# Equal byte offsets for TensorE's operands, value products of two heads at once, and stages in another order

## The chip, the core and the metric

One Trainium2 chip; the kernel runs on one of its cores. The metric is device microseconds from launch to end of the whole program, as the median of several runs. TensorE (PE) multiplies into PSUM, VectorE (DVE), ScalarE (ACT) and GpSimd (POOL) do elementwise work, and SyncE (SP), ACT and POOL issue DMA transfers from queues of their own.

## The reference

One decoder layer on a sequence of 1024 tokens of width 1024, all in float32.

```
u    = rmsnorm(x) * (1 + scale(c)) + shift(c)
proj = u @ w_in                       # a, b, conv_gate: 1024 columns each; q, k, v, ret_gate: 1024 each
conv = silu(layernorm(causal_conv31(a * sigmoid(b)))) @ conv_pw * silu(conv_gate)
q, k = rotary(q), rotary(k) / 16      # 4 heads of 256
r    = retention(q, k, v)             # per head, with decay, in chunks of tokens
ret  = head_groupnorm(r) * silu(ret_gate)
h    = x + gate(c) * (concat(conv, ret) @ w_out)
out  = rmsnorm(h) * final_g
```

## The kernel before

Every float32 operand of a product is split into a high part in TensorE's float32r format and a low remainder (`split`: a ScalarE copy and a subtraction). A product is then three matmuls per 128 rows of contraction: high by high, high by low, low by high (`mm3`, lines 81 to 83). One of the two operands is stationary (the weights of the matmul instruction, 128x128), the other streams through (the moving operand, 128x512 or 128x256).

The work runs in stages, each of which leaves intermediate results in DRAM buffers (`d_y`, `d_v`, `d_qk`, ...):

- **Head** (`head`): loads, the RMS norm, transposes, the modulation from c, and four 128-column products that start while u is still being made (`ps_e`, `ps_paa` to `ps_pdd`). Then two more products, w_s (`ps_s`), whose weights are split on POOL (`lo_s`).
- **Pairs** (`pair`): the rest of the projection with a seven-product scheme over 2x2 blocks (tiles `pa`, `pb`, `pd`; weights `ph`, `pl`; moving operands `uh`, `ul`, `th`, `tl`). DVE meanwhile runs the convolution, 30 tap instructions per channel tile (`conv_taps`, L263), for eight tiles; the last one, `y7`, is worked on when the pairs are done.
- **Values of head 0** (`values_ps`, tiles `ps_v`, weights `wvh`, `wvl`), stored to `d_v` and loaded back.
- **Retention** (`retention`), for four heads in four chunks each: loads of q, k, v and the gate, splits of them on ACT and DVE (`qch`/`qcl`, `kch`/`kcl`, `vch`/`vcl`), scores `sp`, output `op`, state update `up`, group norm, transposes `tp`. All its matmuls have 256 or 128 moving columns, and each chunk is a chain over PE, DVE, ACT and POOL.
- Between the heads stand the **values of the next head** (`values`), after head 0 the statistics of the layer norm (`ln_stats`: each of the eight rows of `d_y` is loaded, shifted by the mean, stored again, squared and summed; then 1/sqrt and a broadcast `rbs`), and after head 2 the normalisation `norm_z` of those rows, which makes zh and zl in the buffers that uh and ul held.
- **Pointwise** products (`pointwise`, tiles `ps_pw`) of zh and zl, and the **output** products (tiles `ps_o`, and `ps_ol` for the last 128 tokens).

The order on each engine is made when the program is built: the Tile planner takes instructions by priority (the order of the code, shifted by `high_priority` offsets) and puts each on its engine in one fixed sequence. An engine then runs its sequence strictly in order. The addresses in SBUF follow from the pools' order and sizes.

Of the kernel before, what the change touches and what calls it, by code (L numbers as in the profile page):

```python
# [7 lines left out]
F32 = mybir.dt.float32  # L8
F32R = mybir.dt.float32r
# [14 lines left out]
PAD_RIGHT = 8  # L24
# [22 lines left out]
def hybrid_layer(ctx: ExitStack, tc: tile.TileContext, x, vec, c_row, ada_ss, ada_g, adab_g, w_e, w_s, w_p, w_v,  # L47
# [17 lines left out]
    d_v = dram.tile([H, P, TT, 2 * P], F32, name="d_v")  # L65
# [62 lines left out]

    pad_p = ctx.enter_context(tc.tile_pool(name="pad", bufs=1, side="right"))
    pad_p.tile([P, PAD_RIGHT], F32, name="pad")  # L130
# [14 lines left out]
    def head():  # L145
# [104 lines left out]
        return ps  # L250

    def conv_taps(m, ap=None, yp=None):

        with tc.high_priority(offset=-TAPS_LATER):
# [11 lines left out]
            nc.sync.dma_start(d_y[m], y)  # L266
# [16 lines left out]
    def values_ps(ws, name):  # L283

        for tg in range(2):
            ps = [mmp.tile([P, 2, 2 * P], F32, tag="mm", name=f"ps_{name}{tg}{i}") for i in range(2)]
            for k in range(KT):
                wh, wl = ws[k]
                for j in range(4):
                    sl = slice((4 * tg + j) * P, (4 * tg + j + 1) * P)  # L290
                    mm3(ps[j // 2][:, j % 2], uh[k][:, sl], ul[k][:, sl], wh, wl,
                        k == 0 and j % 2 == 0, k == KT - 1 and j % 2 == 1)
            for i in range(2):
                yield 2 * tg + i, ps[i]

    early = head()
# [26 lines left out]
    for j, n in enumerate(STD):  # L323
        ps = unit(*load_w(w_s[j], [P, KT, P], f"s{n}", sw, nc.gpsimd), uh, ul, f"s{n}")
        if j == 0:
            gate_out(n, ps)
# [5 lines left out]
    with tc.tile_pool(name="one", bufs=1, reuse_waits="tile") as op_, \  # L332
# [162 lines left out]
        for h in range(1):  # L495
            ws = []
            for j in range(4):
                raw = op_.tile([P, HK, P], F32, tag="raw", name=f"wv{h}{j}", bufs=6)
                nc.sync.dma_start(raw, w_v[h, j // 2][:, 2 * (j % 2):2 * (j % 2) + 2].rearrange(
                    "p k (a c) -> p (k a) c", a=2))  # L500
                hi = op_.tile([P, HK, P], F32R, tag="ph", name=f"wvh{h}{j}", bufs=7)
                lo = op_.tile([P, HK, P], F32R, tag="pl", name=f"wvl{h}{j}", bufs=7)
                split(hi, lo, raw, nc.gpsimd)
                ws += [(hi[:, 2 * i:2 * i + 2], lo[:, 2 * i:2 * i + 2]) for i in range(2)]
            for n, ps in values_ps(ws, f"v{h}"):
                vs = snap(ps, f"v{h}{n}")
                nc.scalar.dma_start(d_v[h, :, 2 * n:2 * n + 2], vs.rearrange("p (t e) -> p t e", t=2))
# [6 lines left out]
    with tc.tile_pool(name="ret", bufs=1, reuse_waits="tile") as rp, \  # L514
            tc.tile_pool(name="retps", bufs=1, space=bass.MemoryType.PSUM) as rps:

        def ln_stats():
# [7 lines left out]
            for m in range(KT):  # L525
# [6 lines left out]
                else:  # L532
                    sq = fo.tile([P, S], F32, tag="xh", name=f"sq{m}", bufs=2)
                    nc.scalar.activation(sq, yt, AF.Square)
                    nc.vector.tensor_tensor(ysum, ysum, sq, op=ADD)
            var = mmp.tile([P, TT], F32, tag="mm", name="var")
# [15 lines left out]
        def values(h):  # L552
            ws = [load_w(w_v[h, g], [P, 4, 2 * P], f"v{h}{g}", wpool) for g in range(2)]
            ws = [(ws[k // 4][0][:, k % 4], ws[k // 4][1][:, k % 4]) for k in range(KT)]
# [123 lines left out]
        def pointwise(m):  # L678
# [3 lines left out]
            for i in range(2):  # L682
                sl = slice(i * HALF, (i + 1) * HALF)
                nc.vector.tensor_tensor(cg[:, sl], ps[i], cg[:, sl], op=MUL)  # L684
# [214 lines left out]
```

## Time and profile before

| | |
|---|---|
| median of 3 runs | 1012.49 us (1011.83 to 1013.82) |
| the profiled execution | 1015.1 us, of it 1013.3 us from the first to the last instruction (the span) |
| PE busy in the span | 961.0 us, 95% |
| DVE, ACT, POOL busy | 741.1, 412.4, 379.9 us |
| mean granted TensorE clock | 0.975 |

Matmuls overlap: a record of a 512-column matmul lasts about 0.39 us while the next starts about 0.23 us after it. So PE's busy share says whether matmuls follow each other, and the number of matmuls in a stretch says how fast. Times inside the execution are counted from the span's start.

### The profile page before, as it was taken

The numbers are of one execution on the slowest core, as the hardware profiler recorded it, in microseconds if no ns is written. First come the engines' busy times: TensorE is split into PE (matmuls) and PEld (weight loads), VectorE is DVE, ScalarE is ACT, GpSimd is POOL, SyncE is SP. The second block draws the span as 40 slices with busy tenths as digits, with TensorE's granted clock in tenths as the row PEclk, the third lists the DMA queues.
The fourth block names the chain that finished last, engine by engine and source line by source line (L and its number), as shares of the span: only waits on it lengthen the run. The fifth ranks groups of instructions, "written<-read, shape, count | busy, mean of one in ns | idle before, by whom it ended". The sixth has DMA issues, their size and how long they took to land.

```text
span 1013.3 us, 13308 instructions
## 1 busy us (share of the span) xinstructions
PE 961.0 (95%) x4880; PEld 812.2 (80%) x4880; DVE 741.1 (73%) x926; ACT 412.4 (41%) x676; POOL 379.9 (37%) x347
## 2 busy tenths in 40 slices
PE   7899999999999999999977977899999999999997
PEld 5687788888888888888877966899888878888886
DVE  6989889898999999999799569536785354422322
ACT  7754443434333342433334556546742323211110
POOL 3201989878879778877402010101101000000000
PEclk9999999999999999999997996899999999999999
DMA  9712333324243353352256577445776577332111
GB/s 358 295 63 73 104 115 135 114 83 144 93 138 118 112 181 105 103 167 94 96 178 208 189 255 261 173 146 185 219 258 236 191 243 225 125 104 84 62 42 42
DMA packets 83827, 154.99 MB, mean 153 GB/s; under 512 B 6705, under 2 KB 40241, under 8 KB 82610
## 3 DMA queue, kind: packets, MB, share of 16 engines
q1 hardware_dynamic: 81026, 148.64, 44.2%
q10 hardware_dynamic: 2736, 5.51, 1.4%
q8 instruction: 38, 0.62, 0.3%
q14 instruction: 27, 0.22, 0.1%
HBM read 107.99 MB, written 46.14 MB: 152 GB/s over the span
## 4 chain that ended last, share of the span: by engine, by line
PE 32%; DMA 9%; DVE 7%; ACT 2%; issue 2%; POOL 0%; POOLq 0%; DVEq 0%; ACTq 0%; SPq 0%
PE ps_o L83 5%; PE ps_o L81 5%; PE ps_o L82 5%; DVE y L263 3%; PE ps_pw L81 2%; PE ps_pw L83 2%; PE ps_pw L82 2%; PE ps_v L81 1%; PE ps_v L82 1%; PE ps_v L83 1%; DMA v<-d_v 1%; DMA yt<-d_y 1%; DMA ys<-d_y 1%; DMA d_y<-ys 1%; DMA d_v<-vs 1%
## 5 line engine op out<-in xcount | busy, mean ns | idle before, releaser
L263 DVE SCALAR_TENSOR_TENSOR yp<-a,vec_t,yp 128x1024 f32<-128x1024 f32 x210 | 269.5, 1283 | 11.5 <-ACT yp L261 7.1
L371 POOL TENSOR_TENSOR pl<-pr,ph 128x512 fp32r<-128x512 f32 x63 | 83.4, 1332 | 94.4 <-ACT ph L370 90.7
L371 POOL TENSOR_TENSOR pl_s<-sm_s,ph_s 128x512 fp32r<-128x512 f32 x63 | 85.7, 1362 | 29.2 <-ACT ph_s L370 26.1
L370 ACT CAST ph_s<-sm_s 128x512 fp32r<-128x512 f32 x63 | 39.0, 622 | 105.8 <-PE pa L82 99.6
L650 POOL TENSOR_TENSOR rs<-mv,kc_t 128x2 f32<-128x2 f32 x16 | 5.5, 344 | 202.1 <-DVE mv L647 171.3
L772 POOL TENSOR_TENSOR fr<-fr,mhalf 128x1 f32<-128x1 f32 x7 | 3.8, 544 | 198.8 <-DVE fr L771 198.8
L370 ACT CAST ph<-pr 128x512 fp32r<-128x512 f32 x63 | 38.8, 622 | 75.7 <-PE pa L82 33.7
L81 PE MATMUL pa<-th,ph_s 128*128 128x512 f32 x168 | 66.1, 393 | 1.0 <-ACT ph_s L370 1.0
L83 PE MATMUL pa<-th,pl_s 128*128 128x512 f32 x168 | 66.2, 394 | 0.7 <-POOL pl_s L371 0.7
L82 PE MATMUL pa<-tl,ph_s 128*128 128x512 f32 x168 | 65.8, 392 | 0.0
L81 PE MATMUL pb<-uh,ph_s 128*128 128x512 f32 x168 | 65.4, 389 | 0.0
L83 PE MATMUL pb<-uh,pl_s 128*128 128x512 f32 x168 | 65.4, 389 | 0.0
L82 PE MATMUL pb<-ul,ph_s 128*128 128x512 f32 x168 | 65.4, 389 | 0.0
L376 POOL TENSOR_TENSOR sm_s<-pr,pr 128x512 f32<-128x512 f32 x42 | 56.4, 1344 | 4.1 <-PE pa L83 2.2
L81 PE MATMUL ps_v<-hi_v,uh 128*128 128x256 f32 x192 | 54.7, 287 | 0.9 <-ACT hi_v L69 0.9
L83 PE MATMUL ps_v<-hi_v,ul 128*128 128x256 f32 x192 | 55.5, 290 | 0.0
L82 PE MATMUL ps_v<-lo_v,uh 128*128 128x256 f32 x192 | 55.0, 287 | 0.0
L763 DVE TENSOR_TENSOR g<-ps_o,gate 128x512 f32<-128x512 f32 x14 | 9.7, 691 | 60.4 <-PE ps_o L83 60.3
L82 PE MATMUL ps_pw<-zl,hi_pw 128*128 128x512 f32 x128 | 50.8, 398 | 0.1
L83 PE MATMUL ps_pw<-zh,lo_pw 128*128 128x512 f32 x128 | 50.8, 399 | 0.0
L81 PE MATMUL ps_pw<-zh,hi_pw 128*128 128x512 f32 x128 | 50.3, 399 | 0.3 <-DVE cgl L684 0.3
L81 PE MATMUL ps_o<-woh,hi_yr 128*128 128x512 f32 x112 | 44.7, 399 | 0.0
(440 smaller groups left out, 2910.7 us busy)
## 6 DMA issues: line engine op xcount, KB each, us to landing
pr<-w_p SPq DMA_DIRECT2D x84, 256.0 KB, 2.7
aw<-ada_ss SPq DMA_DIRECT2D x8, 1024.0 KB, 8.0
d_qk<-ro SPq DMA_DIRECT2D x16, 512.0 KB, 3.1
wo<-w_out SPq DMA_DIRECT2D x16, 512.0 KB, 4.6
xt<-x SPq DMA_DIRECT2D x8, 512.0 KB, 6.5
d_y<-y SPq DMA_DIRECT2D x8, 512.0 KB, 3.4
d_sg<-o SPq DMA_DIRECT2D x16, 256.0 KB, 2.1
q<-d_qk SPq DMA_DIRECT2D x16, 256.0 KB, 4.1
```

The source lines that it names most:

```text
L81: nc.tensor.matmul(ps, lh, rh, start=start, stop=False, skip_group_check=more)
L82: nc.tensor.matmul(ps, lh, rl, start=False, stop=False, skip_group_check=more)
L83: nc.tensor.matmul(ps, ll, rh, start=False, stop=stop, skip_group_check=more)
L263: nc.vector.scalar_tensor_tensor(acc, ap[:, j:j + S], col(V_CW, m * CW + j), acc, op0=MUL, op1=ADD)
L370: nc.scalar.copy(hi, src)
L371: nc.gpsimd.tensor_tensor(lo, src, hi.bitcast(F32), op=SUB)
L376: nc.gpsimd.tensor_tensor(out, a, b, op=op)
L650: nc.gpsimd.tensor_tensor(rs, mv[:, :, 1], kc_t[:, K_G2 + 2 * h:K_G2 + 2 * h + 2], op=MUL)
L763: nc.vector.tensor_tensor(g[:, :n], ps(), gate[:, sl], op=MUL)
L772: nc.gpsimd.tensor_tensor(r, r, mhalf[:, 0:1], op=ALU.pow)
```

## The change

Five things are done at once.

1. **Addresses.** Pools are padded and opened in another order, and placeholder tiles come first in the retention's pool, so that both operands of every float32r matmul start at one offset within 512 bytes. In the two built programs these offsets are:

| products | stationary, before | moving, before | after, both |
|---|---|---|---|
| early head products (`ps_e` and the others of the head) | 320 | 128 | 128 |
| `ps_s` | 192 | 128 | 128 |
| pairs, retention, values of head 0 | 128 | 128 | 128 |
| values of heads 1 to 3 | 128 | 448 | 128 |
| `ps_pw`, `ps_o`, `ps_ol` | 448 | 128 | 128 |

2. **Values.** w_v is laid out for two heads at a time, so one product has 512 moving columns instead of 256: 384 matmuls in place of 768. The values of heads 0 and 1 are all made after the pairs (192 matmuls, weights in th and tl, which the last pair has done with), those of heads 2 and 3 in two halves after heads 0 and 1.
3. **Order of the stages.** The layer norm's squares stay after head 0, its scale and `norm_z` come after head 1 instead of heads 0 and 2, and the pointwise products follow on from there.
4. **Loads and stores.** w_s comes in one load after most of the head's loads, into a buffer of the head. The values of heads 0 and 1, and the last row of `d_y`, are stored from POOL's queue.
5. **The gate** (`gate_step`) is written after the first output tile, and its product takes PSUM from another pool.

```diff
-PAD_RIGHT = 8
+PAD_SW = 24
+PAD_W = 88
...
-    d_v = dram.tile([H, P, TT, 2 * P], F32, name="d_v")
+    d_v = dram.tile([2, P, TT, HALF], F32, name="d_v")
...
+    whp = head_ctx.enter_context(tc.tile_pool(name="wh", bufs=2))
     hp = head_ctx.enter_context(tc.tile_pool(name="head", bufs=1))
-    whp = head_ctx.enter_context(tc.tile_pool(name="wh", bufs=2))
...
+    xs_p.tile([P, PAD_SW], F32, name="pads")
...
+        raw = hp.tile([P, len(STD), D], F32, tag="aw", name="raw_s", bufs=3)
+        nc.sync.dma_start(raw, w_s)
+        ws = []
+        for j, n in enumerate(STD):
+            hi = sw.tile([P, KT, P], F32R, tag="hi", name=f"hi_s{n}")
+            lo = sw.tile([P, KT, P], F32R, tag="lo", name=f"lo_s{n}")
+            split(hi, lo, raw[:, j].rearrange("p (k c) -> p k c", k=KT), nc.gpsimd)
...
-            nc.sync.dma_start(d_y[m], y)
+            (nc.gpsimd if yp is None else nc.sync).dma_start(d_y[m], y)
...
+    def values_ps(t, ws, name):
+
+        ps = mmp.tile([P, HALF], F32, tag="mm", name=f"ps_{name}{t}")
+        sl = slice(t * P, (t + 1) * P)
+        for k in range(KT):
+            mm3(ps, uh[k][:, sl], ul[k][:, sl], *ws[k], k == 0, k == KT - 1)
+        return ps
...
+        for k in range(KT):
+            raw = op_.tile([P, HALF], F32, tag="raw", name=f"wv0{k}", bufs=6)
+            nc.sync.dma_start(raw, w_v[0, k // 2][:, k % 2])
+            hi, lo = (t[:, k % HK] for t in ((th[2], tl[2]), (th[3], th[4]))[k // HK])
+            split(hi, lo, raw, nc.gpsimd)
+            ws.append((hi, lo))
+        for t in range(0, TT, 2):
+            vs = op_.tile([P, 2, HALF], F32, tag="ro", name=f"vs0{t}", bufs=2)
+            for i in range(2):
+                ps = values_ps(t + i, ws, "v0")
+                if t + 2 < TT:
+                    nc.scalar.copy(vs[:, i], ps)
+                else:
+                    nc.vector.tensor_copy(vs[:, i], ps)
+            values_out(0, t, vs, nc.gpsimd)
...
+    pad_p = ctx.enter_context(tc.tile_pool(name="pad", bufs=1, side="right"))
+    pad_p.tile([P, PAD_W], F32, name="padw")
...
+        for tag, n, dt, bufs in (("vs", HALF, F32, 3), ("state", HALF, F32, 1), ("sth", HALF, F32R, 2),
+                                 ("stl", HALF, F32R, 2), ("ob", HALF, F32, 2), ("rn", CH, F32, 2), ("yn", CH, F32, 2),
+                                 ("sh", 3 * P, F32R, 2), ("sl", 3 * P, F32R, 2), ("sm", 3 * P, F32, 1),
+                                 ("gap", P, F32, 1)):
+            rp.tile([P, n], dt, tag=tag, name=f"first_{tag}", bufs=bufs)
...
+        def values(ts):
+
+            if not w_v1:
+                for j in range(4):
+                    hi, lo = load_w(w_v[1, j], [P, 2, HALF], f"v1{j}", wpool)
+                    w_v1.extend((hi[:, i], lo[:, i]) for i in range(2))
+            for t in ts:
+                vs = rp.tile([P, 1, HALF], F32, tag="vs", name=f"vs{t}", bufs=3)
+                nc.scalar.copy(vs[:, 0], values_ps(t, w_v1, "v1"))
+                values_out(1, t, vs, nc.scalar)
...
         for h in range(H):
             retention(h)
-            if h < H - 1:
-                values(h + 1)
+            if h < 2:
+                values(range(h * HK, (h + 1) * HK))
             if h == 0:
-                rbs = ln_stats()
-            if h == H - 2:
+                ln_squares()
+            if h == 1:
+                rbs = ln_scale()
                 for m in range(KT):
                     zh[m], zl[m] = norm_z(m)
```

Three places of the built programs' order matter below. The first is DVE at the border between the pairs' stage and the retention; `y7` are taps of the last convolution tile, `q00`, `k00`, `v00` belong to head 0, chunk 0. Before:

```order
L263 SCALAR_TENSOR_TENSOR y7_2389<-a7_2386,vec_t_75,y7_2389 128x1024 x11
L70 TENSOR_TENSOR qcl00_4641<-q00_4613,qch00_4640 128x512
L70 TENSOR_TENSOR vcl00_4622<-v00_4619,vch00_4621 128x512
L263 SCALAR_TENSOR_TENSOR y7_2389<-a7_2386,vec_t_75,y7_2389 128x1024
L70 TENSOR_TENSOR kcl00_4637<-k00_4615,kch00_4636 128x512
```

In the changed program DVE's rows there are:

```order
L271 SCALAR_TENSOR_TENSOR y7_2384<-a7_2381,vec_t_75,y7_2384 128x1024 x17
L516 COPY vs06_4551<-ps_v06_4552 128x512
L516 COPY vs06_4551<-ps_v07_4578 128x512
L71 TENSOR_TENSOR vcl00_4647<-v00_4644,vch00_4646 128x512
L71 TENSOR_TENSOR qcl00_4666<-q00_4638,qch00_4665 128x512
L71 TENSOR_TENSOR kcl00_4662<-k00_4640,kch00_4661 128x512
```

All taps now stand ahead of the retention's first split, and between them the two copies of the last value tiles.

The second place is PE at the start of head 1 (`sp10` are scores of head 1, chunk 0). Before, transposes of head 0 and the next chunk's scores follow:

```order
L82 MATMUL sp10_5412<-qcl10_5409,kch10_5404 128x128
L660 MATMUL tp03_5041<-ident_t_76,rn030_5042 128x128 x2
L660 MATMUL tp03_5041<-ident_t_76,rn031_5046 128x128 x2
L83 MATMUL sp10_5412<-qch10_5408,kcl10_5405 128x128
L592 MATMUL kp10_5395<-ident_t_76,k10_5383 128x128 x2
L81 MATMUL sp11_5522<-qch11_5518,kch11_5514 128x256
```

In the changed program value products of heads 2 and 3 (`ps_v14`, then `ps_v15`) follow, 29 matmuls in a row, of which these are the first:

```order
L84 MATMUL sp10_5312<-qch10_5308,kcl10_5305 128x128
L82 MATMUL ps_v14_5726<-hi_v10_5084,uh0_94 128x512
L83 MATMUL ps_v14_5726<-lo_v10_5085,uh0_94 128x512
L84 MATMUL ps_v14_5726<-hi_v10_5084,ul0_102 128x512
L82 MATMUL ps_v14_5726<-hi_v10_5084,uh1_95 128x512
```

So independent products now stand inside head 1; over that head they are 96 matmuls of 512 columns.

The third place is SP's queue in the head. Before, the two loads of w_s stand ahead of the fourth `aw` load:

```order
L157 DMA aw_394<-ada_ss 128x2048
L297 DMA kc_t<-kc 128x24
L74 DMA raw_s_705<-w_s 128x1024
L74 DMA raw_s_765<-w_s 128x1024
L157 DMA aw_434<-ada_ss 128x2048
```

In the changed program the one load stands behind the eighth:

```order
L157 DMA aw_591<-ada_ss 128x2048
L162 DMA wer_553<-w_e 128x512
L251 DMA raw_s<-w_s 128x2048
L162 DMA wer_593<-w_e 128x512
L372 DMA pr_11_909<-w_p 128x512
```

The split of w_s moves with it: POOL makes `lo_s` when the seventh of the eight u tiles is being made, not the second.

## Rows read from the trace of the kernel before

**Rows 1.** Busy time in chosen stretches: us, instructions (x), granted TensorE clock, DMA.

```profile
core 0: us, PE busy (x) PEld busy (x) DVE busy (x) ACT busy (x) POOL busy (x), PEclk, DMA share, GB/s
120.00:490.00 370.00, 370.00 (x1634) 306.39 (x1633) 352.45 (x353) 144.04 (x242) 298.91 (x228) 1.00 0.37 120
508.00:524.00 16.00, 16.00 (x135) 16.00 (x135) 15.71 (x16) 4.05 (x8) 0.00 (x0) 1.00 0.62 194
525.00:552.00 27.00, 15.06 (x88) 13.65 (x87) 25.14 (x37) 10.92 (x20) 4.49 (x5) 0.75 0.62 205
525.00:827.00 302.00, 270.77 (x1737) 243.70 (x1735) 194.92 (x337) 149.61 (x246) 34.28 (x66) 0.93 0.64 213
587.00:650.00 63.00, 46.79 (x274) 41.54 (x273) 46.99 (x92) 35.52 (x64) 9.72 (x18) 0.78 0.76 261
650.00:712.00 62.00, 61.76 (x524) 61.56 (x524) 32.73 (x62) 34.94 (x58) 4.78 (x13) 1.00 0.46 145
655.00:669.00 14.00, 14.00 (x122) 14.00 (x121) 3.20 (x5) 4.27 (x8) 0.00 (x0) 1.00 0.35 112
792.00:824.00 32.00, 32.00 (x139) 25.79 (x138) 14.65 (x17) 10.75 (x11) 0.00 (x0) 1.00 0.74 250
827.00:984.00 157.00, 157.00 (x673) 126.34 (x672) 52.76 (x63) 30.54 (x46) 3.27 (x6) 1.00 0.35 116
984.00:1013.30 29.30, 22.25 (x145) 19.87 (x143) 8.55 (x17) 3.80 (x11) 1.27 (x3) 0.96 0.09 36
```

**Rows 2.** DVE in order of time, 490 to 552 us: start, us, tile, count.

```profile
515.87 14.48 DVE L263 SCALAR_TENSOR_TENSOR y<-a,vec_t,y 128x1024 f32<-128x1024 f32 x11
530.27 0.69 DVE L70 TENSOR_TENSOR qcl<-q,qch 128x512 fp32r<-128x512 f32 x1
...
543.26 1.27 DVE L263 SCALAR_TENSOR_TENSOR y<-a,vec_t,y 128x1024 f32<-128x1024 f32 x1
```

**Rows 3.** The chain that ended last, in order of time: start, us, step.

```profile
551.69 0.74 PE ps_v L81 x4
...
591.67 1.15 DVE ys L528
592.84 6.37 DMA d_y<-ys
599.26 5.21 DMA ys<-d_y
```

**Rows 4.** DVE in order of time: last square added, and rows normalised.

```profile
631.71 1.21 DVE L535 TENSOR_TENSOR ysum<-ysum,sq 128x1024 f32<-128x1024 f32 x1
...
650.52 2.36 DVE L671 TENSOR_TENSOR yt<-yt,rbs 128x1024 f32<-128x1024 f32 x2 [2.51 <-ACT rbs L549]
...
706.84 2.35 DVE L671 TENSOR_TENSOR yt<-yt,rbs 128x1024 f32<-128x1024 f32 x2
```

**Rows 5.** The instructions of line 671 (`norm_z`): count, ns, first start to last end.

```profile
L671 DVE TENSOR_TENSOR yt<-yt,rbs x8: 1218/1225/1227, 650.5 to 735.1; 128x1024 f32<-128x1024 f32 x8
```

**Rows 6.** DVE in order of time in the head.

```profile
30.64 3.38 DVE L206 TENSOR_TENSOR ul<-xs,uh 128x1024 fp32r<-128x1024 f32 x1
34.05 2.75 DVE L309 TENSOR_TENSOR xs<-xs 128x512 f32<-128x512 f32 x1
...
39.13 1.22 DVE L206 TENSOR_TENSOR ul<-xs,uh 128x1024 fp32r<-128x1024 f32 x1
...
40.87 0.68 DVE L309 TENSOR_TENSOR xs<-xs 128x512 f32<-128x512 f32 x1
```

**Rows 7.** POOL in order of time in the head.

```profile
30.50 5.76 POOL L70 TENSOR_TENSOR lo_s<-raw_s,hi_s 128x1024 fp32r<-128x1024 f32 x2 [11.21 <-ACT hi_s L69]
```

**Rows 8.** PE's waits, 15 to 115 us: in total, times, longest.

```profile
PE ps_e L82 <- DVE ul L206: 3.0, 2, 2.9
```

**Rows 9.** DMA issues: KB each, median us from issue to landing.

```profile
v<-d_v SPq DMA_DIRECT2D x16, 256.0 KB, 3.6
...
d_v<-vs ACTq DMA_DIRECT2D x12, 256.0 KB, 3.1
```

More of the change, by code (lines that the diff above doesn't have):

```diff
@@ L281, in conv_early, with values_out @@
         return ap
[L283 to L296, printed above, removed]
+    def values_ps(t, ws, name):
[4 more added lines that the diff above has]
+        return ps
+    def values_out(g, t, vs, eng):
+        eng.dma_start(d_v[g, :, t:t + vs.shape[1]], vs)
+    early, w_std = head()
     nc.sync.dma_start(kc_t, kc)
@@ L550, in ln_stats @@
             return rbs
-        def values(h):
-            ws = [load_w(w_v[h, g], [P, 4, 2 * P], f"v{h}{g}", wpool) for g in range(2)]
-            ws = [(ws[k // 4][0][:, k % 4], ws[k // 4][1][:, k % 4]) for k in range(KT)]
-            for n, ps in values_ps(ws, f"v{h}"):
-                vs = rp.tile([P, 2, 2 * P], F32, tag="vs", name=f"vs{h}{n}", bufs=2)
-                nc.scalar.copy(vs, ps)
-                nc.scalar.dma_start(d_v[h, :, 2 * n:2 * n + 2], vs)
+        w_v1 = []
+        def values(ts):
[7 more added lines that the diff above has]
+                values_out(1, t, vs, nc.scalar)
         def retention(h):
@@ L725, in load_y @@
             return load_w(src[:, :, t * P:(t + 1) * P].rearrange("f p s -> p f s"), [P, KT, P], f"{n}{t}", wpool)
-        agb = fo.tile([P, D], F32, tag="yt", name="agb", bufs=2)
-        nc.sync.dma_start(agb, adab_g.broadcast_to([P, D]))
-        for i in range(2):
-            sl = slice(i * HALF, (i + 1) * HALF)
-            gp = fps.tile([P, HALF], F32, tag="o", name=f"gp{i}")
-            nc.tensor.matmul(gp, ones_t, gate[:, sl], start=True, stop=True)
-            nc.vector.tensor_tensor(gate[:, sl], gp, agb[:, sl], op=ADD)
         w_r = [load_r(KT + f, fp, "r2", 16) for f in range(KT)]
@@ L798, in hybrid_layer @@
             half(ps, w_c, load_y(d_yc, t, "yc"), False)
+            if t == 0:
+                for k in range(KT):
+                    gate_step(k)
+                agb = fo.tile([P, D], F32, tag="yt", name="agb", bufs=2)
+                nc.sync.dma_start(agb, adab_g.broadcast_to([P, D]))
+                for i in range(2):
+                    sl = slice(i * HALF, (i + 1) * HALF)
+                    gp = mmp.tile([P, HALF], F32, tag="mm", name=f"gp{i}")
+                    nc.tensor.matmul(gp, ones_t, gate[:, sl], start=True, stop=True)
+                    nc.vector.tensor_tensor(gate[:, sl], gp, agb[:, sl], op=ADD)
             finish(t, [(lambda q=q: q, sl) for q, sl in zip(ps, halves2)])
@@ L869, in _layout @@
         "w_p": c(np.stack([[w_m[n][:, j:j + HK] for n in ms for j in (0, HK)] for _, *ms in PAIRS])),
-        "w_s": c(w_m[list(STD)]),
+        "w_s": c(np.stack([w_m[n].reshape(P, D) for n in STD], axis=1)),
         "w_v": c(w_v),
```

65 lines of the change are left out of this document (26 added, 39 removed).

## The prediction

> **What bounds the kernel now.** I read the page's busy shares first (PE 95%, DVE 73%), then busy time by stretch [rows 1], and there not PE's share but matmuls per us. In the pairs' stage 1,634 records of 512 columns overlap 370 us; less two cut at the edges, one starts every 0.2267 us, without a gap. In the output stage 673 overlap 157 us: 157/671 = 0.2340. In the pointwise stage 139 overlap 32 us: 32/137 = 0.2336. All three stretches have the full clock, PE waits in none of them, and yet two of them are 3% slower for each matmul. DMA share doesn't explain it: the output stage moves as little as the pairs (0.35 against 0.37). What differs, as far as I see, is the table of offsets: equal in the pairs, 320 bytes apart in the other two (448 and 128).
>
> Then come stretches where PE isn't full. From 525 to 552 only 88 matmuls overlap 27 us, at clock 0.75; from 587 to 650 it is 274 in 63 us, at 0.78. At the pace of the full stretch behind it (524 in 61.76 us, 0.118 each) they are 10.4 and 32.3 us of work: 16.6 and 30.7 us lost, **47 in all**. The chain of waits names the reasons. From 525 PE has only head 0's chunks, each a chain over four engines, and DVE still has 17 taps of `y7`, which the planner mixes with the chunks' splits; the last tap begins at 543.26 [rows 2]. From 591.67 the chain goes `ys`, store (6.37 us), load (5.21 us) [rows 3]: the layer norm's rounds, one for two rows of `d_y`, four in all. The last square is added by 632.9, so a round takes (632.9 - 591.67)/4 = 10.3 us; `rbs` is ready at 650.5 [rows 4]. PE does nothing in the rounds; head 1 alone, at a reduced clock, is what it has beside them.
>
> **The change, part by part.** *Pitch.* 384 `ps_pw` and 672 `ps_o` matmuls and 48 `ps_ol` of 512 columns go from 0.234 to 0.2267 if the offsets are the cause: 1,104 x 0.0073 = 8.0 us. With 256 columns the rows go the other way: 0.1203 where equal (508 to 524: 16/133), 0.1167 where 320 apart (655 to 669: 14/120) [rows 1]. So the 96 narrow `ps_ol` give back 0.4. The values were 192 x 0.1203 + 576 x 0.1167 = 90.3 us; as 384 wide ones they are 87.1: 3.2 less. For the head's 288 products I take 1.2 us. Sum: **12 us**. Lower bound 3 (only the values' width counts), upper 13.
>
> *w_s later.* `lo_s` ran on POOL for 5.76 us from 30.50 [rows 7]. In that time a `ul` on DVE took 3.38 us, the next of its kind 1.22, and an `xs` 2.75 for 0.68 [rows 6]; PE waited 2.9 us for that `ul` [rows 8]. With `lo_s` at the seventh u tile DVE is slowed there instead, where PE has more products ready. PE gains 0 (it waits later) to 3.7 us; I take **1.8**, half.
>
> *Border of pairs and retention.* The pairs' share of matmuls ends where it did; v0 before took 192 x 0.1203 = 23.1 us up to 524.7, so it began at 501.6. Now twice the product: 192 x 0.2267 = 43.5, to about 545.1. DVE has its taps in one piece: 17 from 515.87 at 14.48/11 = 1.316 end at 538, under PE's values. Behind v0 stand the copy of the last value tile, the store and load back of `v00`, its split, then scores. The store took 3.1 us, the load 3.6 [rows 9]; the copies, splits and scores of a first chunk I take from rows like [rows 2] (0.5 to 0.7 each) as some 8 us in which PE has little. First product of the next values (551.69 before [rows 3]) then at about 553: PE idles 8 us and not 16.6, and 43.5 us instead of 23.1 of values are done. **Gain 9**; 0 if the chunks' chain runs as thinly as before, 14 if the planner's filling works at once.
>
> *Where the stores are issued.* The values' store and `y7`'s go to POOL's queue. No row of before shows a DMA issued by POOL, so its price is bounded by 3.1 us (an ACT store) and 6.37 (`d_y`'s worst step). The longer one, on the last tile alone, costs 3 us. I take 0: the earlier tiles are stored while PE makes the later ones. POOL's queue has almost nothing else between 525 and 552 (5 instructions).
>
> The Trainium skill, SBUF — State Buffer, section "SBUF: two separate sides", speaks against this edit: a DMA issued from GpSimd's queue gets its descriptors written by GpSimd, which is locked out of a port pair it shares with VectorE while that runs a two-port instruction. No run here shows it so far. If the taps held back every value store until 538, v00's store and load would end at 538 + 3.1 + 3.6 = 544.7, still ahead of v0's end at 545.1, so by that rule the sum would change by at most a us.
>
> *Head 0 and head 1.* Before, the first shifted row begins at 591.67, 40 us after the first value product at 551.69 [rows 3]. From 553 that would be 593; but of the 10.4 us of matmuls that ran ahead of 552 I let 4 fall behind it: 597. From the first `ys` to `rbs` it was 58.8 us; the rounds are DMA and DVE work, which the change doesn't shorten, but DVE is done with `y7`, and the end of the chain needs PE, at a better clock: 45 to 59, I take 52, `rbs` at **649**. What stands for PE between the mean's matmul and the broadcast, by the order of rows: before 222 matmuls of head 1, about 22 us; now 96 of the values (21.8 us) and 173 of head 1, about 38 us. The stretch was 63 us (587 to 650) and is 57 (592 to 649): 41 us without work become 19, **gain 22**. If this cover is used up before the rounds end, the values' 21.8 us only change places.
>
> *Norm and pointwise.* `norm_z` has four steps of two rows. The first began at 650.5, the other three ran from 706.84 to 735.1 [rows 4, 5], 9.4 us each; between lay the wait for `uh` and `ul`, which values(3) still read. That wait is gone: four steps and some 4 us for the last split, z7 at about 691. By PE's order there are 4 us of work between the broadcast and the first pointwise product, and 126 between that and the first output product: 384 x 0.2267 = 87.1 of pointwise, 39 of retention. The first two pointwise tiles need all of z; with them (96 x 0.2267 = 21.8) and head 2 (some 20) PE has 42 us for the 42 up to z7, so I charge 4 us of waits. Output begins at 649 + 130 + 4 = **783** (826.8 before). There it is 672 x 0.2267 = 152.3 us, and the last stage stays at 29.3 + 0.4 [rows 1]: 965. The head's 3 us (1.8, and 1.2 of pitch) come off: **962** for the span.
>
> Stage by stage, after less before: up to v0's end 542.1 - 524.7 = +17.4; to the next values 8 - 27 = -19; to `rbs` 96 - 98.8 = -2.8; to the first output product 134 - 176.3 = -42.3; output -4.9, end +0.4: **-51**. By cause that is 12 of pitch and width, 2 of w_s, 9 at the border, 22 beside the rounds; the other 6 are thin places of heads 0, 2 and 3. 1013.3 - 51 = 962. The profiled execution was 1015.1 and 2.6 above the median 1012.49, the span 0.8 above it; I put the median at the span, 962.
>
> **Rivals.** *A. The stalls remain.* PE's sequence is fixed when the program is built, and an engine waits at each instruction in it: 29 value matmuls in a row at head 1's start can use up the cover before the slow rounds, and the 17 taps ahead of the first split make DVE late for head 0. For it: head 1's chain is shortest when DVE is free, and from 587 to 650 DMA was already 0.76 busy [rows 1]. Then pitch and head remain: 1013 - 14 = 999.
> *B. PE is the bound from the values on.* The rounds run at 8 us each instead of 10.3, and head 1 fills what is left: of the 8 + 19 + 4 us without work half goes, 962 - 15 = 947. Against it: each chunk's chain needs four engines, and the rounds before ran at the DMA's pace.
> *C. Slower.* 525 to 827 moved 213 GB/s x 302 us = 64 MB [rows 1]. The same bytes now have some 258 us, 249 GB/s on the mean, where the busiest stretch had 261. If that throttles the norm's eight rounds (four of statistics, four of `norm_z`), which nothing longer covers, each 6.4 us more eats the 51; that is the point from which it decides. At 8 us more: 962 + 64 = 1026. Against it: most of these transfers are weights fetched ahead, which can wait.
> *D. The offset is not the cause of the pitch.* Output and pointwise stay at 0.234: 962 + 8 = 970. Against it: equal clock and DMA share in the two stretches, and that narrow matmuls differ by offset too, in the other direction, which a traffic reason would not give.
>
> **How the numbers follow.** Likeliest 0.60 (own range 950 to 976: rounds 50 to 64, border 0 to 14), A 0.15 (990 to 1004), B 0.15 (935 to 953), C 0.05, D 0.05. The range 944 to 986 holds the likeliest, D and two thirds of B; it leaves out A, C and a rest of B, 0.2. A difference of 0.2%, 2 us, is about what a measurement can tell here from none. All cases but C are faster: 0.95. C I split: 0.02 within 0.2%, 0.03 slower.
>
> **What the changed profile would show.** Output stage: 672 matmuls at 0.227 (0.234 speaks for D), 152 us long. In the head all `ul` near 1.2 us up to `lo_s`, and the long ones where `lo_s` runs. From 525 to 545 PE full with `ps_v0`, taps through by 538. `rbs` near 649 with some 20 us without work ahead of it; first output product near 783. For POOL's stores, time from issue to landing near 3 us. I am wrong if a DMA share above 0.8 lasts through head 1 and `norm_z` with PE waiting for `yt` or `ys` loads (C), if the clock stays low from 550 to 650 with as few matmuls as before (A), or if retention starts far behind 553, since `v00` came late from POOL's queue.

## The result, and the profile after

The changed kernel takes **985.08 us** (median of 4 runs, 982.69 to 988.71) against 1013.12 of the kernel before beside it: ratio 0.9728, interval [0.9693, 0.9762], 28 us faster. Run a second time it gave 0.9755 [0.9721, 0.9788]. Forecast were 962 and a range of 944 to 986: the gain is there, a little over half of what was expected, and the two medians (985.08 and, the second time, 987.32) lie on either side of the range's upper end. The profiled execution took 983.87 us, its span is 982.1.

Busy time by stretch, columns as in [rows 1]:

```profile
120.00:490.00 370.00, 370.00 (x1634) 306.43 (x1633) 348.14 (x350) 144.25 (x242) 296.67 (x226) 1.00 0.37 123
525.00:552.00 27.00, 24.09 (x113) 20.57 (x113) 23.28 (x28) 8.67 (x15) 4.04 (x4) 0.87 0.51 178
587.00:643.00 56.00, 51.67 (x314) 45.44 (x313) 42.22 (x77) 34.46 (x59) 9.77 (x13) 0.97 0.85 293
643.00:791.00 148.00, 141.34 (x787) 121.83 (x785) 97.64 (x181) 74.40 (x123) 20.13 (x40) 0.97 0.61 203
791.00:827.00 36.00, 32.04 (x129) 24.36 (x128) 18.32 (x17) 13.54 (x13) 0.00 (x0) 0.95 0.83 264
830.00:950.00 120.00, 119.94 (x529) 98.98 (x529) 39.92 (x51) 22.79 (x38) 3.27 (x6) 1.00 0.31 101
952.00:982.00 30.00, 22.51 (x145) 20.43 (x143) 8.50 (x17) 3.81 (x11) 1.28 (x3) 0.94 0.09 36
```

Read it against [rows 1]. The pairs are what they were. From 525 to 552 PE is busy 24 us, not 15. From the mean to `rbs` it was 63 us with 274 matmuls, now 56 with 314, and many of them are wide. In the later part of the output stage 529 records overlap 120 us: 527 starts, 0.2277 us each, so the 0.234 of before is gone. But the first 36 us of that stage hold 129 records where that pace gives 158, and this stretch of before had no such hole. What PE waits for there, 788 to 960 us:

```profile
PE ps_o L82 <- ACT woh L70: 4.2, 4, 2.0
```

`woh` is the high part of an output weight. Right behind the longest of these waits the granted clock stands at 0.5 (1.2 GHz), and seven matmuls in a row start 0.43 us or more apart instead of 0.227; by the starts around them that is about 1.7 us more:

```profile
807.90:811.20 3.30, 3.30 (x10) 2.27 (x8) 1.74 (x2) 1.04 (x1) 0.00 (x0) 0.50 0.96 285
```

SP's queue tells why `woh` is late (start us, us, queue, line, transfer):

```profile
781.83 0.37 SPq L691 DMA_DIRECT2D d_yr<-sg  x1
782.25 0.87 SPq L774 DMA_DIRECT2D h<-x  x1
783.17 0.91 SPq L743 DMA_DIRECT2D wo<-w_out  x2
790.07 2.06 SPq L743 DMA_DIRECT2D wo<-w_out  x2
```

The first two output weights are asked for at 783, eight us ahead of the first output product (790.99), and each further load waits for one of two raw buffers. Ahead of them stand stores of the retention's gated results (`d_yr`) and of the pointwise results (`d_yc`), for whose data SP waited (735 to 830 us: in total, times, longest):

```profile
SPq L691 <- DVE sg L690: 15.5, 3, 12.3
SPq L721 <- DVE cgl L720: 14.4, 4, 8.8
```

The 12.3 us belong to the last chunk but one, whose store is issued at 766.55, and the 8.8 to the `d_yc` store at 779.22; the last chunk's own store, at 781.83, waited 2.2. Of the 27.6 us ahead of that store SP waited 25.9.

By its own places the forecast compares so (times in the profiled execution; forecast less the 3 us of the head):

| place | forecast | measured |
|---|---|---|
| last product of v0 ends | 542.1 | 540.9 |
| first product of the next values | 550 | 552.0 |
| mean's matmul | 589 | 588.7 |
| `rbs` ready | 646 | 643.1 |
| last `zl` done | 688 | 688.5 |
| first output product | 780 | 791.0 |
| output stage up to `ps_ol` | 152.3 | 161.0 |
| from there to the end | 29.7 | 30.1 |

So up to z the way was right, within 3 us. Two terms failed: 148 us instead of 134 from `rbs` to the output, and 8.7 us more in the output stage. The rest of the study asks whether the parts that look right were right for the reasons given, and where those two terms come from.

### The profile page after: what moved, and what is told of

Same layout as the page of the kernel before. It is cut to its first block, busy times and chain, and to the rows that moved or that the text cites. A ratio compares the mean times of both kernels' runs of the same rounds, so it can differ in the third digit from the quotient of the medians.

```text
span 982.1 us, 12550 instructions
## 1 busy us (share of the span) xinstructions
PE 942.8 (96%) x4496; PEld 786.4 (80%) x4496; DVE 742.7 (76%) x926; ACT 410.4 (42%) x676; POOL 395.6 (40%) x356
## 4 chain that ended last, share of the span: by engine, by line
PE 79%; DMA 8%; DVE 5%; issue 3%; ACT 2%; POOL 1%; SPq 0%; POOLq 0%; DVEq 0%; ACTq 0%
PE pa L84 8%; PE pa L83 8%; PE pa L82 8%; PE ps_o L83 4%; PE ps_o L84 4%; PE ps_o L82 4%; PE pb L84 4%; PE pb L82 4%; PE pb L83 4%; DMA wo<-w_out 3%; PE ps_v L82 2%; PE ps_v L83 2%; PE ps_v L84 2%; PE pd L82 2%; PE pd L84 2%
## 5 line engine op out<-in xcount | busy, mean ns | idle before, releaser
L271 DVE SCALAR_TENSOR_TENSOR yp<-a,vec_t,yp 128x1024 f32<-128x1024 f32 x210 | 269.6, 1284 | 15.0 <-ACT yp L269 11.1
L378 POOL TENSOR_TENSOR pl_s<-sm_s,ph_s 128x512 fp32r<-128x512 f32 x63 | 83.3, 1326 | 25.3 <-ACT ph_s L377 21.3
L271 DVE SCALAR_TENSOR_TENSOR y<-a,vec_t,y 128x1024 f32<-128x1024 f32 x30 | 44.4, 1480 | 6.6 <-ACT y L269 5.8
L83 PE MATMUL ps_o<-wol,hi_yr 128*128 128x512 f32 x112 | 44.6, 398 | 0.1
L84 PE MATMUL ps_o<-woh,lo_yr 128*128 128x512 f32 x112 | 44.1, 396 | 0.0
L83 PE MATMUL ps_o<-wol,hi_yc 128*128 128x512 f32 x112 | 44.0, 393 | 0.1
```

The lines of the kernel that those rows point to most:

```text
L83: nc.tensor.matmul(ps, lh, rl, start=False, stop=False, skip_group_check=more)
L84: nc.tensor.matmul(ps, ll, rh, start=False, stop=stop, skip_group_check=more)
L271: nc.vector.scalar_tensor_tensor(acc, ap[:, j:j + S], col(V_CW, m * CW + j), acc, op0=MUL, op1=ADD)
L378: nc.gpsimd.tensor_tensor(lo, src, hi.bitcast(F32), op=SUB)
```

## Experiments

All ratios are to the kernel before in runs on the same chip. A difference to the changed kernel is given as a span, from its two ratios, 0.9728 and 0.9755.

### The pitch: one pad away, one pad put in

```diff
-PAD_W = 88
+PAD_W = 8
```

> The changed kernel with only the pad ahead of the pointwise and output weights back at its old size: stationary and moving operands of ps_pw, ps_o and ps_ol again 192 bytes apart (mod 512), those of the values of heads 2 and 3 320 apart; no instruction in another place. Offset theory (mine): output and pointwise matmuls start 0.234 to 0.235 us apart instead of 0.227, 1,104 x 0.0075 = 8 us more matmul time; the output stage of the changed kernel waits some 7 us for its weights, and slower matmuls can hide in these waits, so 3 to 8 us slower than the changed kernel, 986 to 993 us. Rival (the pitch comes from the traffic or the stage, case D): pitch 0.227 as in the changed kernel, time within 2 us of it.

Measured 991.09 us, ratio 0.9806 [0.9777, 0.9836]. In the kernel before the opposite edit:

```diff
+    pad_w = ctx.enter_context(tc.tile_pool(name="padw", bufs=1, side="right"))
+    pad_w.tile([P, 80], F32, name="padw")
     wpool = ctx.enter_context(tc.tile_pool(name="w", bufs=4, side="right", reuse_waits="tile"))
```

> The kernel before with one pad of 320 bytes ahead of the weights of values, pointwise and output, so that both operands of these products start at one offset; no instruction in another place. Offset theory: pointwise and output matmuls go from 0.234 to 0.227 us, 1,104 x 0.0073 = 8 us gained; the 576 narrow value matmuls go from 0.1167 to 0.120 and the 96 narrow ps_ol from 0.113 to 0.120, 2.5 us lost; together 5 to 8 us faster than before, 1005 to 1008 us. Rival (case D): no change, within 2 us.

Measured 1005.61 us, ratio 0.9945 [0.9923, 0.9967]: by the ratio 5.6 us faster. The output stage without waits, first the changed kernel with the old pad, then the kernel before with the new one:

```profile
830.00:950.00 120.00, 119.66 (x512) 96.11 (x513) 41.18 (x51) 22.96 (x39) 3.27 (x6) 1.00 0.31 101
```

```profile
827.00:978.00 151.00, 151.00 (x667) 125.00 (x666) 52.41 (x63) 31.09 (x46) 3.27 (x6) 1.00 0.37 121
```

510 starts in 120 us are 0.235, 665 in 151 are 0.227, at the same clock and DMA share as in the kernel that each is compared with. No instruction stands elsewhere in either pair of kernels, so the address alone sets the pitch, as forecast; case D is refuted both ways. Of the time, the old pad's price in the changed kernel lies at 5 to 8 us by the two ratios of the changed kernel, but their intervals touch; the pitch is the firm part.

### w_s early

The head loads w_s as before (`load_w` of each half, split on POOL, at the place of use).

> The changed kernel with w_s loaded and split as before, in two loads that stand ahead of the fourth load of the modulation. If POOL's split of w_s is what slows VectorE in the head: one ul of about 3.4 us and an xs of 2.7 beside lo_s, PE waits some 3 us for it, and the end of the head comes 1.8 us (0 to 3.7) later than in the changed kernel. Rival: PE is held elsewhere in the head anyway, and nothing moves (within 0.7 us at the start of the pairs).

Measured 989.84 us, ratio 0.9793 [0.9763, 0.9824]. In this kernel VectorE has the pattern of [rows 6] and PE that of [rows 8]:

```profile
30.27 3.38 DVE L206 TENSOR_TENSOR ul<-xs,uh 128x1024 fp32r<-128x1024 f32 x1
33.69 2.75 DVE L308 TENSOR_TENSOR xs<-xs 128x512 f32<-128x512 f32 x1
```

```profile
PE ps_e L83 <- DVE ul L206: 3.1, 2, 2.9
```

In the changed kernel `lo_s` runs from 53.42, and then it is other instructions of VectorE that are slow, a weight split (0.69 us elsewhere) and a modulation sum (1.22):

```profile
53.59 2.90 DVE L166 TENSOR_TENSOR wel<-wer,weh 128x512 fp32r<-128x512 f32 x1
56.41 3.41 DVE L193 SCALAR_TENSOR_TENSOR junk<-aw,cbc 128x1024 bf16<-128x1024 f32 x1
```

```profile
53.42 5.32 POOL L71 TENSOR_TENSOR lo_s<-raw_s,hi_s 128x1024 fp32r<-128x1024 f32 x2 [34.40 <-ACT hi_s L70]
```

```profile
PE ps_e L83 <- DVE ul L206: 2.4, 1, 2.4
```

The stall is not removed but moved: PE waits 2.4 us for the seventh `ul`, which stands behind the slow instructions, not 2.9 for the second. The other us or two of the head come from the granted clock. The first execution of the changed kernel and its second one differ from 60 to 68 us by that alone:

```profile
60.00:68.00 8.00, 6.38 (x28) 5.26 (x29) 7.00 (x10) 4.54 (x6) 0.00 (x0) 1.00 0.00 0
```

```profile
60.00:68.00 8.00, 6.30 (x21) 5.07 (x22) 7.08 (x10) 4.51 (x5) 0.00 (x0) 0.79 0.00 0
```

and reach the first pair product at 94.5 and 96.1. ws_early reaches it at 96.0, within what the changed kernel does. So w_s late is worth some 0.5 us by its waits, not the 1.8 I took. The whole of ws_early is 4 to 7 us slower by the ratios, with an interval that overlaps that of the changed kernel's second run, and its profiled execution (988.32 us) is no longer than that of the changed kernel's second run (988.64). What w_s costs beyond the head stays open.

### The stores' queue

The value stores of heads 0 and 1 on ACT's queue and `y7`'s on SP's, and then `y7`'s alone:

```diff
-            (nc.gpsimd if yp is None else nc.sync).dma_start(d_y[m], y)
+            nc.sync.dma_start(d_y[m], y)
...
-            values_out(0, t, vs, nc.gpsimd)
+            values_out(0, t, vs, nc.scalar)
```

> The changed kernel with the value stores of heads 0 and 1 on ACT's queue and y7's store on SP's, as before. My price for the POOL queue was 0 to 3 us: time within 2 us of the changed kernel, v0's first chunk no earlier than 549. Rival A (POOL's stores land later, held back by VectorE): the first scores of head 0 come 1 to 3 us earlier here. Rival B (a store in ACT's sequence holds up what is behind it): 1 to 5 us slower here.

> The changed kernel with one store moved: that of y7 is issued from SP's queue, the value stores stay on POOL's. Theory (the y7 store, which waits for the last tap at 538, stands ahead of all of head 0's loads in SP's queue): k, q, v of chunk 0 issued behind 537.5 instead of at 516 to 519, PE waits 5 to 8 us for k, the mean's matmul at 594 to 598 instead of 588.7 to 592, time as stores_hw or 1 us less: 4 to 8 us slower than the changed kernel. Rival (the value stores, which stood 11 us in ACT's sequence, were what cost): mean at 589 to 592, time within 2 us of the changed kernel.

Measured 991.53 us, 0.9810 [0.9779, 0.9841] for both, and 994.91 us, 0.9852 [0.9825, 0.9880] for `y7` alone. SP's queue of the second:

```profile
539.44 0.32 SPq L274 DMA_DIRECT2D d_y<-y  x1
539.81 0.42 SPq L589 DMA_DIRECT2D mask<-masks  x1
540.32 0.74 SPq L603 DMA_DIRECT2D sg<-d_sg  x1
541.16 0.50 SPq L603 DMA_DIRECT2D v<-d_v  x1
541.71 0.59 SPq L603 DMA_DIRECT2D q<-d_qk  x1
542.35 0.60 SPq L603 DMA_DIRECT2D k<-d_qk  x1
```

and of the changed kernel:

```profile
515.73 0.37 SPq L603 DMA_DIRECT2D v<-d_v  x1
516.14 0.59 SPq L603 DMA_DIRECT2D q<-d_qk  x1
516.79 0.60 SPq L603 DMA_DIRECT2D k<-d_qk  x1
```

What SP and PE wait for there with `y7`'s store on SP's queue:

```profile
SPq L274 <- DVE y L271: 31.8, 1, 31.8
```

```profile
PE kp L617 <- DMA k<-d_qk: 5.9, 1, 5.9
```

The store waits 31.8 us for the last tap, and all loads of head 0 stand behind it. The mean's matmul comes at 597.2 and 597.8 in these two kernels, 588.4 to 592.1 in the changed kernel and all that keep its stores there and its w_s, but for values_together below. So of the parts of the change this line, priced at 0 to 3 us of loss, is worth some 6 to 12 us of gain. That is more than the 4 to 8 that I expected of y_store_sp, and stores_hw was expected within 2 us. The value stores on ACT add no loss to it.

### The order of the stages

```diff
             if h == 0:
                 ln_squares()
-            if h == 1:
                 rbs = ln_scale()
+            if h == 2:
                 for m in range(KT):
```

> The changed kernel with the layer norm's scale after head 0 and norm_z after head 2, as before; values, loads, addresses as in the changed kernel. My theory: rbs comes at about the same time (640 to 652), because it hangs on the four rounds; z comes later, so heads 2 and half of 3 run without pointwise products beside them, and more of these are left for the end. That costs 5 to 20 us between rbs and the first output product, and gives back the 7 us of weight waits in the output stage, as there is time for these loads again: 0 to 13 us slower than the changed kernel. Rival (the order of the stages is what the gain hangs on): 20 us or more slower.

Measured 997.78 us, 0.9858 [0.9833, 0.9882]: some 10 to 13 us slower than the changed kernel. And all values of heads 2 and 3 after head 0 (`values(range(TT))`):

> The changed kernel with all values of heads 2 and 3 after head 0, none after head 1. Theory (the value products are the cover of the rounds): the products stand ahead of the mean instead of beside the rounds; mean some 15 to 22 us later, from the mean to rbs 45 to 55 us with as few matmuls as before, 5 to 20 us slower than the changed kernel. Rival (the planner puts them where there is room, and only priorities change): within 3 us.

Measured 998.98 us, 0.9868 [0.9841, 0.9895], 11 to 14 us slower. From the mean to `rbs`, old order first, then the values together:

```profile
590.00:651.00 61.00, 43.65 (x247) 38.11 (x246) 44.17 (x86) 33.46 (x58) 10.09 (x17) 0.80 0.71 243
```

```profile
616.00:674.00 58.00, 42.60 (x249) 38.47 (x247) 46.85 (x86) 35.63 (x61) 7.66 (x13) 0.76 0.87 282
```

Both have the picture of before ([rows 1], 587 to 650): some 250 matmuls, the clock near 0.78. In both most or all of the value products no longer stand beside the rounds, in the first since the norm's scale is then earlier in the code than the second half of the values. From the mean's matmul to `rbs` 96 of the values' matmuls start in the changed kernel, 17 with the old order and none with the values together. In values_together nothing else was moved in the code: `rbs` comes at 675.9 and the first output product at 810.5, 17 to 20 us later than in the changed kernel, and the output stage, which has its weights earlier there, gives 4 to 6 back. So the cover of the rounds is worth 11 to 14 us in the end. The old order shows it less cleanly, because `norm_z` moves too: `rbs` is 7 to 10 us late (652.6), the stretch behind it 5 us longer (152.8 us). I expected `rbs` at about its old time there and the loss behind it, so the place was wrong. I also expected that the old order would give back the waits for output weights; it doesn't. Its first weight is asked for at 797.31, 8.1 us ahead of the output.

### The two terms that failed

The first two raw tiles of the output weights into `norm_z`'s buffers, so that their loads can stand earlier, and those loads at a higher priority, so that they do:

```diff
-            raw = fp.tile([P, D], F32, tag="rw", name=f"wo{f}", bufs=2)
-            nc.sync.dma_start(raw, w_out[f])
+            raw = (fo.tile([P, D], F32, tag="yt", name=f"wo{f}", bufs=2) if KT <= f < KT + 2 else
+                   fp.tile([P, D], F32, tag="rw", name=f"wo{f}", bufs=2))
+            with tc.high_priority(offset=LOADS_EARLIER if KT <= f < KT + 2 else 0):
+                nc.sync.dma_start(raw, w_out[f])
```

> The changed kernel with the first two raw tiles of the output weights in norm_z's yt buffers, so that their loads stand in SP's queue some fifty rows ahead of the last head's store of sg instead of behind it. Theory (the output stage starts short of weights because their loads stand in SP's queue behind a store that waits 12 us for the last chunk's gate): PE's 7 us of waits in the first 36 us of the output stage shrink to 0 to 3, output stage 153 to 156 instead of 161 us, 4 to 8 us faster than the changed kernel, span 974 to 978. Rival (the two raw buffers pace all sixteen weight tiles, about 4 us each): the waits only move some us later, time within 2 us.

Measured 976.56 us, 0.9647 [0.9623, 0.9671]: 8 to 11 us faster than the changed kernel, more than the 4 to 8 expected. (The store that waits 12 us is, as shown above, not that of the last chunk.) Its queue:

```profile
687.38 0.35 SPq L745 DMA_DIRECT2D wo<-w_out  x1
691.12 0.34 SPq L745 DMA_DIRECT2D wo<-w_out  x1
774.22 0.94 SPq L745 DMA_DIRECT2D wo<-w_out  x2
```

and PE's waits in its output stage, 4.2 us in the changed kernel:

```profile
PE ps_o L82 <- ACT woh L70: 1.5, 1, 1.5
```

The edit moves more than these two loads. The buffers that it takes are also those of the gate's rows, and so the gate's eight steps on DVE run from 785 to 813 us, beside the output products, instead of from 688 to 722, and its product stands inside the output stage instead of just ahead of it. The stage is shorter although it has this work too. But the first output product also comes earlier, 197.2 us behind the mean's matmul instead of 202.3 and 202.8, and whether that is due to the gate's absence from the stretch ahead of it no run separates.

The stores of the retention and of the pointwise stage on POOL's queue:

> The changed kernel with the stores of the retention's gated result (d_yr) and of the pointwise result (d_yc) issued from POOL's queue instead of SP's. Theory (a store that waits at the head of SP's queue for its data holds up the loads behind it, and this thins heads 1 to 3): 5 to 15 us faster than the changed kernel, the stretch from rbs to the first output product 135 to 143 us instead of 148, and shorter waits of the output stage too. Rival (the chunks' chain over four engines sets the pace, and loads come early enough): within 2 us; POOL's own rows, which each chunk needs for its norm, may be held up by the stores and make it up to 5 us slower.

Measured 981.54 us, 0.9702 [0.9673, 0.9732]: 3 to 5 us faster by the ratios, but the intervals overlap, and it is not to be told from the changed kernel. The stretch from `rbs` is 142.7 us, as expected, but only because `rbs` comes late (650.3). The output weights are asked for at 784.96, 8.0 us ahead again, because another row of SP then waits ahead of them (`h`, for a buffer that the store of `d_yc` frees):

```profile
SPq L774 <- DMA d_yc<-cgl: 11.8, 1, 11.8
```

Last the low parts of the pointwise weights on POOL (`load_w(..., wpool, nc.gpsimd)`), alone and with wo_early, and beside them the changed kernel again:

> The changed kernel with the low parts of the pointwise weights (lo_pw, 8 x 1.2 us on VectorE) made on POOL. Theory (VectorE is what thins heads 1 and 2: from 640.65 to 653 it works without a pause, and a lo_pw that waits for its weights stands ahead of head 2's splits): the stretch from rbs to the first output product 141 to 146 us instead of 148, 2 to 7 us faster. Rival (POOL's 2.7 us for each slow VectorE beside it, as lo_s does in the head, where a 1.2 us instruction takes 3.4): 0 to 6 us slower.

> Both: the first two loads of the output weights early, as in wo_early (0.965 of before), and lo_pw on POOL. If the two places are independent, the sum of their differences to the changed kernel: 968 to 975 us by the theory of VectorE, 976 to 982 by its rival. If the output stage needs the pointwise products at the end as cover, the second gain is given back as waits for weights: 974 to 978.

> The changed kernel itself, unchanged, beside the next two. A ratio to before of 0.970 to 0.976. Its head shows whether the end of the head, which lay between 92.0 and 93.9 us in seven runs with the same instructions there, is the same each time: if the granted clock's drop near 61 us comes and goes, 1.5 us of the head belong to the clock and not to w_s.

Measured 977.53 us, 0.9662 [0.9629, 0.9695]; 975.16 us, 0.9635 [0.9608, 0.9663]; 987.32 us, 0.9755 [0.9721, 0.9788]. The first gains 7 to 9 us, the upper end of what my theory of VectorE said or more, but not where it said. `rbs` comes at 650.7, 5.5 us later than in the repeated changed kernel, and the first output product at 794.5, 1 us later; the 143.8 us between them are short only because `rbs` is late. VectorE is slowed beside POOL here too (in the rows, `lo_pw` on POOL, and a `ysum` of VectorE that takes 1.19 us just before):

```profile
631.12 2.57 POOL L71 TENSOR_TENSOR lo_pw<-raw_pw,hi_pw 128x1024 fp32r<-128x1024 f32 x1
```

```profile
631.95 2.83 DVE L553 TENSOR_TENSOR ysum<-ysum,sq 128x1024 f32<-128x1024 f32 x1
```

The gain is in the output stage, whose first weights are asked for at 779.39, 15.1 us ahead. From 794 on, where the stage begins, 36 us hold all 157 records:

```profile
794.00:830.00 36.00, 36.00 (x157) 29.11 (x156) 20.40 (x19) 14.79 (x15) 0.00 (x0) 1.00 0.84 276
```

The two edits together gain 9 to 12 us, hardly more than either alone (8 to 11 and 7 to 9): the first output product stands where wo_early has it (788.0), and the output stage is as long as in pw_split_pool (154.1). Of the expectations for both, 974 to 978 holds, but not for its reason: PE has no waits for weights in the output stage there.

Put together, from the starts of the records (us; the lead is the time from the load to the first output product):

| kernel | first load of output weights | first output product | lead | output stage |
|---|---|---|---|---|
| changed | 783.2 | 791.0 | 7.8 | 161.0 |
| changed_again | 785.6 | 793.5 | 7.9 | 163.3 |
| ret_stores_pool | 785.0 | 793.0 | 8.0 | 162.1 |
| old_ln_order | 797.3 | 805.4 | 8.1 | 161.3 |
| wo_early | 687.4 (third tile 774.2) | 788.0 | 13.8 for the third | 157.0 |
| pw_split_pool | 779.4 | 794.5 | 15.1 | 154.1 |
| wo_early_pw_pool | 688.6 (third tile 770.4) | 788.0 | 17.5 for the third | 154.1 |
| values_together | 792.9 | 810.5 | 17.6 | 157.3 |
| before | 796.2 | 826.8 | 30.6 | 157.2 at 0.234 each |

ws_early, stores_hw and y_store_sp, with leads of 7.9 to 8.2, take 162.2 to 162.8. Above the 152.3 us of 672 x 0.2267, a lead of 8 us costs 9 to 11 us. In pw_split_pool and wo_early_pw_pool the loss is 1.8, no more than the gate's product, which lies inside the stage there (four matmuls 0.43 us apart, 1.7). The lead alone doesn't set the loss: values_together, with 17.6 us, still loses 5.0, of it 1.7 by the gate's product and 1.5 by waits for weights. wo_early moves loads by hand, and PE waits 1.5 us for weights instead of 4.2. So it is shown that late loads are the larger part of this term, not that they are all of it.

## Why the prediction was right, and what it missed

**The time: in part luck.** 985.08 lies 0.9 us inside the range, the second median 1.3 outside. It is in none of the cases' own ranges (950 to 976 for the likeliest, 990 to 1004 for A). The direction is right, and so is the way up to z; what misses are two terms behind it. The chances that the forecast leaves outside its range add up to 0.25 (A 0.15, C 0.05, a third of B 0.05), not 0.2.

**Pitch: right, size too.** The pad alone sets 0.234 or 0.227, in the changed kernel and in the kernel before; 5.6 us [3.3 to 7.8 by its interval] against the 5 to 8 written for the kernel before. The 3.2 us for the values' width were not run alone.

**w_s: the step failed in its kind.** I charged a wait as removed (half of 3.7). It changed its place and became 2.4 us. The forecast said that PE has more products ready at the seventh tile; it had not.

**Border: the sum right, its parts not.** v0's end and the next values came within 2 us of the forecast. But the 8 us between them were charged for the last copy, the store and the load back of `v00`, and these don't stand there: the first chunk's values are stored at 512.56 and asked for at 515.73, 25 us before v0 ends. PE goes on with head 0's first chunk at once and idles 2.9 us of the 11.1, much of the rest at the clock 0.5:

```profile
540.90:552.00 11.10, 8.19 (x43) 7.45 (x42) 9.97 (x17) 5.94 (x10) 0.95 (x2) 0.69 0.80 267
```

That the sum came out is luck. The price of the queue was wrong: I let head 0's loads be as early as before without looking at what stands ahead of them in SP's queue. In the kernel before, `y7`'s store stands behind these loads; with all taps ahead of the splits it would stand in front. POOL's queue keeps that from happening, and is the condition of the gain rather than a cost. On the rule that spoke against it (the Trainium skill, SBUF — State Buffer, section "SBUF: two separate sides": GpSimd can't write descriptors while VectorE holds the shared ports): no run here shows such starvation. The four value stores from POOL took 3.6 us to land at the median, three of them while taps ran on VectorE (2.9 to 5.2; from ACT's queue, in stores_hw, the same three took 2.6 to 3.3):

```profile
d_v<-vs POOLq DMA_DIRECT2D x4, 512.0 KB, 3.6
```

The advice of that section of the Trainium skill, to issue from SP's or ACT's queue instead, cost those 6 to 12 us where `y7`'s store went to SP's queue, for a reason of order and not of ports. It is no sharp test of the rule: taps have two inputs in SBUF, and by the same section such an instruction takes the ports only against a GpSimd instruction that reads SBUF.

**Rounds and cover: right.** `rbs` 643.1 for 646; taking the cover away cost 11 to 14 us in values_together. The 22 us of the forecast were PE work moved beside the rounds; what it won by the end is that smaller number. The sign of some 20 us without work didn't show: from 587 to 643 PE is idle for 4.3 us (16.2 before, 587 to 650), and the matmuls there start further apart than at their pitch.

**From `rbs` to the output: the term was mis-sized, 134 forecast, 148 measured.** My 130 us of work counted every matmul at its undisturbed pitch, and 4 us of waits. By the starts of the records, with what PE waited behind each, the 384 pointwise matmuls there took 91.7 us (87 forecast), the narrow ones 55 (43 forecast), the gate's product 1.3. PE is idle for 6.7 us, most of it in two waits (643 to 791):

```profile
PE kp L617 <- DVE state L660: 2.5, 1, 2.5
PE tp L685 <- ACT rn L683: 2.5, 1, 2.5
```

Around the end of each the clock falls to 0.5 for a while, where matmuls take nearly twice as long; by the distances of the starts that is some 5 us:

```profile
647.50:654.20 6.70, 5.76 (x22) 4.91 (x22) 6.49 (x11) 5.16 (x8) 0.99 (x2) 0.50 0.69 226
746.50:749.70 3.20, 3.09 (x15) 3.09 (x16) 2.84 (x4) 3.20 (x7) 0.00 (x0) 0.50 0.44 176
```

The rest are distances a little over the pitch. So the term had the waits 3 us too small and left out the lower clock behind them. Nor does the stretch hang on `rbs`, as the forecast's sum has it: in the ten traces of kernels that keep the order of the stages and of the values the first output product comes 197 to 204 us behind the mean's matmul, while `rbs` comes 53 to 60 us behind it, and where `rbs` is late the stretch behind it is short. What would shorten it no run shows alone. It isn't SP's queue (200.9 us from the mean in ret_stores_pool, against 202.3 and 202.8), nor the splits of the pointwise weights (203.6 in pw_split_pool); the lowest, 197.2, is wo_early, where the gate's steps have left this stretch. This part stays open.

**The output stage: a cost I didn't charge, 8.7 us.** The forecast carried over the stage's length at the new pitch. In the kernel before, ten of the sixteen loads of weight tiles are issued ahead of the first output product (from 796.2 on, through two raw buffers), beside 30 us of pointwise products; in the changed kernel it is three. The change uses these products to fill heads 2 and 3, and so takes that cover away. Of the 8.7 us, 4.2 are PE's waits for `woh` and about 1.7 the lower clock behind the longest of them; the rest are distances a little over the pitch. It is the question that I asked of the rounds ("if the cover is gone") and didn't ask here. Of the 51 us forecast for the span 20 are missing, 14 + 8.7 less 3 that `rbs` came early. Rival A (stalls remain) describes them, but at other places than it named. B and D don't hold. Of C one sign came, a DMA share of 0.85 from 587 to 643, but not its cost: `rbs` was early.

The best kernel of the study, wo_early_pw_pool, takes 975.16 us, 3.65% less than the kernel before and about 1% less than the changed one; by the intervals it can't be told from wo_early and pw_split_pool.

## What to carry to other kernels

If matmuls that wait for nothing start at different distances in two stages, compare the byte offsets of their operands; a pad is a cheap test. Before using late independent work to fill early gaps, look up what it hid where it stood: here it was the loads of the stage behind it. And a DMA in a queue waits for its own data with everything behind it waiting too, so for each store whose data comes late, read which loads stand behind it, in the order of the changed program and not of the old one.

## What the runs showed of the hardware

float32r matmuls of 512 columns start 0.227 us apart with both operands at one offset within 512 bytes, and 0.234 to 0.235 where they are 192 apart (moving less stationary, 128 - 448, modulo 512; the prediction counts the same pair as 320). With 256 columns it is the other way: 0.120 at one offset, 0.113 at 192 apart (the median of the 96 narrow `ps_ol` of off192). Why, no run tells.

A float32 instruction of VectorE over 1024 columns with both inputs in SBUF takes 1.7 to 3.4 us when it starts beside a running POOL instruction such as a split, 1.2 to 1.3 alone (`ul`, `junk`, `ysum` above, and seven `y7` taps beside the splits of w_v). It ends as if it had waited for POOL's end, to 0.2 us: for the `ysum` above 631.12 + 2.57 + 1.19 = 634.88, and it ends at 631.95 + 2.83 = 634.78. Taps that add up in PSUM (`yp`) are not slowed: 184 of the 210 overlap such a POOL instruction, and none takes more than 1.29 us. The means of the changed kernel (busy us, ns of one | idle before):

```profile
L271 DVE SCALAR_TENSOR_TENSOR yp<-a,vec_t,yp 128x1024 f32<-128x1024 f32 x210 | 269.6, 1284 | 15.0 <-ACT yp L269 11.1
L271 DVE SCALAR_TENSOR_TENSOR y<-a,vec_t,y 128x1024 f32<-128x1024 f32 x30 | 44.4, 1480 | 6.6 <-ACT y L269 5.8
```

The trace agrees with the Trainium skill, SBUF — State Buffer, section "SBUF: two separate sides", which has the shared ports as an exclusive lock for such pairs.
